# A sparse-expert encoder layer: normalised rows laid out by expert and rank while attention runs, instead of gathered by each expert

## The chip, the cores and the metric

One Trainium2 chip, one core. The metric is the device time of one execution in microseconds (us), median of three runs. The core has five engines that run their own instruction streams: TensorE (PE, matrix products), VectorE (DVE), ScalarE (ACT), GpSimd (POOL) and SyncE (SP), which only issues transfers here. Transfers (DMAs) between device memory and on-chip memory are carried by 16 DMA engines. In the profile, transfers issued by SP run on queue q1, those issued by ACT on q10, and those issued by POOL on q0.

## What is computed

One encoder layer on 2048 tokens of width 1024, in fp32: a gated linear attention group (GLA) and a softmax attention group read the same normalised input, their outputs are projected and added to the residual `h`; then a sparse expert layer with 64 experts. Each token goes to the best of 8 groups and to the best 2 of its 8 experts:

```python
g_idx = jnp.argmax(g_logits, axis=-1)
top_val, top_idx = lax.top_k(e_logits, TOP_K)        # 2 of the group's 8 experts
gate = g_w * jax.nn.softmax(top_val, axis=-1)
expert_id = g_idx[:, None] * EXPERTS_PER_GROUP + top_idx
...
h = jax.nn.silu(xb @ w_gate[e]) * (xb @ w_up[e])     # xb: the expert's rows, normalised
return h @ w_down[e]                                 # scaled by gate, added to the residual
```

So there are 4096 assignments of a token to an expert, 64 per expert on average. A final RMS norm ends the layer.

## The kernel before

All products are split products: an fp32 operand is cut into a rounded part (`fp32r`) and a remainder, and three products stand for one. The program has five stages.

- **Projection** (0 to 292 us of the trace): 16 tiles of 128 tokens are normalised, transposed and projected; results go to scratch tensors in device memory.
- **GLA and row maxima** (to 770 us): a loop `for i in range(NT)` (L780) over the 16 tiles. Tile i projects with `wqk` and `wv`, runs the chunked GLA (`gla`, L694) and one pass of row maxima (`maxpass`, L671). `load_u` (L618) loads the next tile's `uT`, `maxpass` loads its `q1`, and GLA's parts are stored (`d_qe`, `d_X`, `d_oi`). The order on every engine is a scheduler's. The remainder of the weights `wv` and the matrix `K1` are loaded by SP at the stage's start.
- **Attention** (to 1640 us): a planner (`Plan`, L120 on) with cost estimates orders PE, DVE, ACT and POOL; SP's order follows the program and the scheduler. Beside the attention blocks (`key_block`) it places each tile's output projection (`project`, L974), which loads the residual into `h`, adds, stores `d_h`, normalises in place, stores the normalised rows to `d_xn`, computes router logits and calls `route` (L1196). `route` finds a token's two experts `eid`, its rank within each expert (`rk`, from a product with a triangular matrix and a running count `acc`), and its gate. A record of token number and gate is scattered by POOL into `d_list` at the place rank x 64 + expert; the last two tiles' records are put into the on-chip table `L` by products (`list_columns`, L1288). `L` has 100 places (`CAP`) for each of 64 experts. The last tile (`last_rows`, L1141; `last_store`, L1190) is spread over steps of its own.
- **Experts** (1690 to 2895 us): `experts` (L1467) plans 64 experts. Each needs six loads of 1 MB by SP (`raw`: two halves each of gate, up and down weights) into 9 buffers; ACT casts each half (`wh`, L1503), DVE makes the remainder (`wl`, L1505), PE multiplies (`products`, L1554). An expert's rows come by `inputs` (L1511): POOL gathers the rows that `L` names out of `d_xn` into one of two buffers `xg` of 100 rows (L1514), PE transposes them (L1540). The result `o` is added into `d_h` by a POOL scatter-add (`sums`, L1609, issue at L1617). The first five weight loads are made at the end of attention; the sixth waits for the first gather:

```python
raws[n] = next_raw(lambda raw: blocks[e][1](raw, which, half), first[0] if after else None)
```

  `first[0]` is the first gather. Names with unused places: a place of `L` that no token holds names a token out of bounds, and the gather skips it.
- **Finish**: `d_h` is read, normalised and written out. A part that runs only if an expert has more than 100 tokens follows; it does not run with these inputs.

A transfer on SP's queue also waits for the transfer eight places before it on its semaphore (eight such semaphores are used in turn by SP and ACT).

Of the kernel before, what the change touches and what calls it, by code (L numbers as in the profile page):

```python
# [8 lines left out]
F32 = mybir.dt.float32  # L9
F32R = mybir.dt.float32r  # L10
I32 = mybir.dt.int32
# [21 lines left out]
LROWS = NE * CAP  # L33
# [163 lines left out]
def hybrid_encoder_kernel(ctx, tc, x, norm1_gain, w_in, gla_up_fwd, gla_up_fwd_bias, gla_up_bwd,  # L197
# [51 lines left out]
    d_h = scratch("d_h", [T, D])  # L249
    d_list = scratch("d_list", [LROWS + OROWS, 2], I32)  # L250
# [5 lines left out]

    nc.gpsimd.dma_start(d_list[0:LROWS].rearrange("(p a) c -> p (a c)", p=CAP), L.rearrange("p e c -> p (e c)"))

# [331 lines left out]
    with ExitStack() as ph:  # L590
# [25 lines left out]
        tset = tc.keep_in_program_order(nc.scalar.preload_act_table_set("natural_log_exp_and_others"))  # L616

# [162 lines left out]
        for i in range(NT):  # L780
            proj(i)
            if i == 0:
                tc.keep_in_program_order(nc.sync.dma_start(K1.bitcast(F32), d_K1))
            if i + 1 < NT:
                load_u(i + 1)
                decay(i + 1)
            else:

                right.close()
                kvp = right.enter_context(tc.tile_pool(name="pkv", bufs=1, side="right", reuse_waits="tile"))  # L790
                K2 = kvp.tile([DH + 1, NKV, T], F32R, name="K2")
                V = kvp.tile([P, NT, NKV, VW], F32R, name="V")
                nc.sync.dma_start(K2.bitcast(F32), d_K2)
                nc.sync.dma_start(V.bitcast(F32), d_V)
                qp = right.enter_context(tc.tile_pool(name="pcq", bufs=2, side="right", reuse_waits="tile"))
                for kv in range(NKV):
                    load_q(NT - 1, kv)
            g, m = gla(i), maxpass(NT - 1 - i)
            while g or m:
                for n, it in ((1, "g"), (2, "m")):  # L800
                    for _ in range(n):
                        if it == "g" and g and next(g, 0) == 0:
                            g = None
                        if it == "m" and m and next(m, 0) == 0:
                            m = None
# [4 lines left out]
    with ExitStack() as ph:  # L810
# [18 lines left out]
                     "h": 1, "gla": 1, "route": 1, "on": 1, "oa": 1, "w": 0, "mtg": 0})  # L829
# [10 lines left out]
        def rsqrt_steps(dst, ss, n, t0):  # L840

            w = ss.shape[-1]
            hx = sp.tile([P, w], F32, name=f"hx{w}", bufs=4)
            t = sp.tile([P, w], F32, name=f"nt{w}", bufs=4)
# [113 lines left out]
        def load_h(i, t, name, bufs):  # L958
            hs = [sp.tile([P, 512], F32, name=name, bufs=bufs) for _ in range(2)]
            for j in range(2):  # L960
                nc.sync.dma_start(hs[j], x2[i * P:(i + 1) * P, j * 512:(j + 1) * 512])
            return hs, landed(t)

        def load_h(i, t, name, bufs):
            hs = [sp.tile([P, 512], F32, name=name, bufs=bufs) for _ in range(2)]
# [8 lines left out]
        def project(i, t):  # L974
# [60 lines left out]
            th = t  # L1035
            for b in range(2):
# [4 lines left out]
                if b == 1:  # L1041
                    give((t[0] + 2.5, "dma"), "h")
# [16 lines left out]
            yield from route(i, lg, t)  # L1059
# [81 lines left out]
        def last_rows(t):  # L1141
# [7 lines left out]
            tx, xs = [], []  # L1149
            for j in range(2):  # L1150
# [4 lines left out]
                tx.append((yield ask("dve", 0.6, t, take=("den",))))  # L1155
                xs.append(sp.tile([P, 512], F32, name="den"))
# [31 lines left out]
            yield from route(i, lg, t)  # L1188
# [7 lines left out]
        def route(i, lg, t):  # L1196
# [53 lines left out]
            t = yield ask("dve", 0.5, t)  # L1250
# [4 lines left out]
            give(t, "pt")  # L1255
            v.tensor_tensor(acc, acc, ob, op=OP.add)
            give(t, f"rank{i - 1}")
            if i in order[-2:]:
# [7 lines left out]
                give(t, "route", "p")  # L1266
                return

            t = yield ask("dve", 0.1, t, tg)
            di = sp.tile([P, 2], I32, name="di", bufs=2)  # L1270
            v.scalar_tensor_tensor(di, rk, float(NE), eid, op0=OP.mult, op1=OP.add)
            give(t, "route")
            for k in range(2):
                t = yield ask("pool", 1.04, t)
# [6 lines left out]
            if i == order[-3]:  # L1281
                t = yield ask("pool", 1.04, t)
                nc.gpsimd.dma_start(L, d_list[0:LROWS].rearrange("(p e) c -> p e c", p=CAP))
                t = yield ask("dve", 0.15, landed(t, 5.0))
                v.tensor_copy(L0, L[:, :, 0])
# [86 lines left out]
        listed = []  # L1372
        last_h, raw_pools, ahead, taken = [], [], [], [0]

        def next_raw(load, after=None):
# [3 lines left out]
            ld = load(raw)  # L1379
            if after is not None:  # L1380
                tc.add_manual_dep(ld.ins, after.ins.name, mybir.DependencyInfo(
                    mybir.DependencyClass.Sync, mybir.DependencyReason.DATA), reason="the first rows go before")
# [31 lines left out]
    with ExitStack() as ph:  # L1414
# [6 lines left out]
        for t in xgs:  # L1421
            nc.gpsimd.memset(t, 0.0)
# [44 lines left out]
        def experts(blocks, ahead=(), then=None):  # L1467
# [3 lines left out]
                         "hh": 2, "o": 2, "visit": NG, "raw": NAHEAD + NB - len(ahead), "issued": 0, "landed": 0})  # L1471
# [11 lines left out]
            def loads():  # L1483
                for n, (e, which, half) in enumerate(seq):
# [3 lines left out]
                    else:  # L1488
                        after = ahead and n == len(ahead)
                        t = yield ask("dma", 2.6, take=("raw", "landed") if after else ("raw",))  # L1490
                        raws[n] = next_raw(lambda raw: blocks[e][1](raw, which, half), first[0] if after else None)
                    give((t[0] + 2.0, "dma"), f"raw{n}")

            def weights(n):
# [11 lines left out]
                if n == 0:  # L1506
                    tc.add_manual_dep(lo.ins, first[1].ins.name, data_dep, reason="the first rows go before")
# [3 lines left out]
            def inputs(e):  # L1511
                xg = xgs[e % 2]
                t = yield ask("pool", 1.95, listed_at, take=("xg",), urge=20.0)
                get = nc.gpsimd.indirect_dma_start(  # L1514
                    out=xg, out_offset=None, in_=d_xn, in_offset=bass.IndirectOffsetOnAxis(ap=column(e, 0), axis=0),
                    bounds_check=T - 1, oob_is_err=False)
                if e == 0:
                    first.extend((get, nc.gpsimd.memset(issued, 0.0)))
                    give(t, "issued")
                t = yield ask("dma", 0.8, (t[0] + 1.5, "pool"), urge=20.0)  # L1520
                if e + 1 < nb:
                    add(inputs(e + 1))
                tx = t[0] + 1.8, "dma"
                if e == 0:
                    give(tx, "landed")
# [112 lines left out]
        with tc.manual_schedule(engines={mybir.EngineType.PE, mybir.EngineType.DVE, mybir.EngineType.Activation,  # L1638
                                         mybir.EngineType.Pool} | ({mybir.EngineType.SP} if SPM & 2 else set())):
            t = experts([(L[:, e], lambda raw, which, half, e=e: load_expert(e, raw, which, half)) for e in expert_order],  # L1640
# [22 lines left out]
        with tc.If(nblk_v > 0):  # L1663
# [19 lines left out]
            with tc.For_i(0, nblk_v, 1) as b:  # L1683
# [9 lines left out]
                experts([(Lb, load)])  # L1693
# [32 lines left out]
```

## Time and profile before

| | |
|---|---|
| median of three runs | 2981.13 us (2977.4 to 2981.16) |
| profiled execution, own time | 2981.33 us |
| its span, first to last instruction | 2979.4 us |
| PE busy | 2812.6 us (94%) |
| DVE, ACT, POOL busy | 75%, 62%, 15% |
| moved by DMA | 647.00 MB, mean 217 GB/s |
| of it queue q1 (SP) | 590.92 MB, 54.3% of 16 engines' span |
| of it queue q0 (POOL) | 34.36 MB, 5.3% |

A share of an engine over the whole span is a mean over stages with different limits, so the rows further down are taken stage by stage. "DMA share" is the mean busy share of the 16 DMA engines, with 1.00 for all busy all the time. PE's granted clock is a share of full speed.

### The profile page before, as it was taken

Reading aid. Unit: us, or ns where it says so; the run is one execution under the profiler, and the core shown is the slowest. Engines: PE = TensorE matmul, PEld = TensorE weight load, DVE = VectorE, ACT = ScalarE, POOL = GpSimd, SP = SyncE. Lnnn points to the kernel's source line nnn. Section 1 sums busy time; section 2 is a strip of 40 time slices with the busy share of each in tenths; the row PEclk is TensorE's granted clock in tenths of the full one; section 3 lists DMA queues with packets and bytes.
Section 4 is the critical chain, followed back from the end, with each engine's and each line's share of the span. In section 5 each row is a group of like instructions: output and inputs, shape, how many; then the busy total and the mean of one; then the engine's idle time right before and its main releaser. Section 6 shows DMA issues by size and latency. Waiting matters only on the chain.

```text
span 2979.4 us, 38648 instructions
## 1 busy us (share of the span) xinstructions
PE 2812.6 (94%) x13776; PEld 2101.0 (71%) x13776; DVE 2225.4 (75%) x3222; ACT 1852.0 (62%) x2776; POOL 448.4 (15%) x326
## 2 busy tenths in 40 slices
PE   7999899999999999999999799999999999999992
PEld 6888688887677777777776566676676666666771
DVE  6655688888676677776666788888788878778783
ACT  4433333333677777777776567777777777777773
POOL 3433111111000000000000121111111112122111
PEclk9999999999899999999999899999999999999996
DMA  7884422233521121121221799999999999999986
GB/s 254 283 279 162 149 105 91 94 105 118 198 66 63 63 80 59 61 80 58 66 77 42 249 371 365 358 355 353 352 364 353 354 353 357 350 345 357 353 311 236
DMA packets 175140, 647.00 MB, mean 217 GB/s; under 512 B 38885, under 2 KB 53575, under 8 KB 119325
## 3 DMA queue, kind: packets, MB, share of 16 engines
q1 hardware_dynamic: 136766, 590.92, 54.3%
q0 software_dynamic: 23712, 34.36, 5.3%
q10 hardware_dynamic: 14464, 19.21, 2.0%
q8 instruction: 109, 1.79, 0.2%
q14 instruction: 89, 0.73, 0.1%
HBM read 546.08 MB, written 117.13 MB: 223 GB/s over the span
## 4 chain that ended last, share of the span: by engine, by line
PE 59%; DMA 21%; issue 7%; DVE 6%; ACT 5%; POOL 1%; ACTq 0%; SPq 0%; POOLq 0%; DVEq 0%
DMA raw<-in_w_gate_dram 10%; DMA raw<-in_w_up_dram 7%; PE pm L1007 6%; PE pm L681 4%; PE pa L1356 4%; PE ps L1328 4%; PE pa L1354 4%; PE pa L1355 4%; PE py L1575 4%; PE pg L1569 4%; PE ps L1329 4%; PE pv L334 3%; PE pqk L334 3%; DVE wl L1505 2%; ACT wh L1503 2%
## 5 line engine op out<-in xcount | busy, mean ns | idle before, releaser
L1505 DVE TENSOR_TENSOR wl<-raw,wh 128x2048 fp32r<-128x2048 f32 x384 | 873.5, 2289 | 218.2 <-ACT wh L1503 215.6
L1503 ACT CAST wh<-raw 128x2048 fp32r<-128x2048 f32 x384 | 727.0, 1908 | 272.5 <-DMA raw<-in_w_up_dram 146.9
L1343 DVE TENSOR_TENSOR p_l<-p,p_h 128x512 fp32r<-128x512 f32 x512 | 343.8, 689 | 199.4 <-ACT p_h L1340 193.1
L1332 ACT ACTIVATE p<-ps 128x512 f32<-128x512 f32 x512 | 296.4, 599 | 150.0 <-PE ps L1329 129.4
L683 DVE TENSOR_REDUCE nm<-pm 128x1 f32<-128x1024 f32 x256 | 304.9, 1216 | 46.7 <-PE pm L681 46.5
L1569 PE MATMUL pg<-wh,xT 128*100 128x512 f32 x1024 | 335.4, 398 | 0.0
L1569 PE MATMUL pu<-wh,xT 128*100 128x512 f32 x1024 | 330.7, 394 | 0.0
L1575 PE MATMUL py<-wh,hT 128*100 128x512 f32 x1024 | 320.7, 416 | 0.0
L1340 ACT CAST p_h<-p 128x512 fp32r<-128x512 f32 x448 | 269.0, 624 | 5.8
L1514 POOL DMA_INDIRECT xg<-d_xn,L x64 | 109.2, 1707 | 914.6 <-PE pt L1540 904.5
L1569 PEld LDWEIGHTS pu<-wh,xT 128*100 128x100 f32 x1024 | 168.1, 164 | 68.2
L1569 PEld LDWEIGHTS pg<-wh,xT 128*100 128x100 f32 x1024 | 170.7, 167 | 64.6
L1328 PE MATMUL ps<-q,K 128*128 128x512 f32 x512 | 210.6, 411 | 1.2 <-ACT p L1332 0.8
L1575 PEld LDWEIGHTS py<-wh,hT 128*100 128x100 f32 x1024 | 170.3, 176 | 55.6
L1354 PE MATMUL pa<-p_h,V 128*66 128x512 f32 x512 | 204.3, 399 | 0.0
L1356 PE MATMUL pa<-p_l,V 128*66 128x512 f32 x512 | 202.6, 396 | 0.9 <-DVE p_l L1343 0.9
L1329 PE MATMUL ps<-q,K 65*128 65x512 f32 x512 | 203.2, 397 | 0.0
L1569 PE MATMUL pg<-wl,xT 128*100 128x512 f32 x512 | 202.0, 395 | 0.0
L1355 PE MATMUL pa<-p_h,V 128*64 128x512 f32 x512 | 201.4, 393 | 0.0
L1569 PE MATMUL pu<-wl,xT 128*100 128x512 f32 x512 | 200.5, 392 | 0.0
L681 PE MATMUL pm<-K,q 128*128 128x512 f32 x512 | 169.6, 416 | 1.1 <-DVE nm L683 1.1
L1575 PE MATMUL py<-wl,hT 128*100 128x512 f32 x512 | 166.3, 407 | 0.0
(415 smaller groups left out, 5041.9 us busy)
## 6 DMA issues: line engine op xcount, KB each, us to landing
raw<-in_w_gate_dram SPq DMA_DIRECT2D x128, 1024.0 KB
raw<-in_w_up_dram SPq DMA_DIRECT2D x128, 1024.0 KB
raw<-in_w_down_dram SPq DMA_DIRECT2D x128, 1024.0 KB
d_uT<-uT SPq DMA_DIRECT2D x16, 1024.0 KB
uT<-d_uT SPq DMA_DIRECT2D x15, 1024.0 KB
x_t<-in_x_dram SPq DMA_DIRECT2D x16, 512.0 KB
wraw<-in_w_in_dram SPq DMA_DIRECT2D x32, 256.0 KB
d_q<-q ACTq DMA_DIRECT2D x16, 512.0 KB
```

The lines of the kernel that those rows point to most:

```text
L683: nc.vector.tensor_reduce(nm[:, h, b:b + 1], pm, axis=AX.XY, op=OP.max, negate=True)
L1328: nc.tensor.matmul(ps, lhsT=K1[:, kv, ks], rhs=r1, start=True, stop=False)
L1329: nc.tensor.matmul(ps, lhsT=K2[:, kv, ks], rhs=r2, start=False, stop=True)
L1332: nc.scalar.activation(p, ps, AF.Exp)
L1343: nc.vector.tensor_tensor(p_l, p, p_h.bitcast(F32), op=OP.subtract)
L1354: nc.tensor.matmul(pa, lhsT=hi, rhs=p_h, start=(kt == 0), stop=False)
L1355: nc.tensor.matmul(pa[0:DH], lhsT=V[:, kt, kv, 0:DH], rhs=p_h, start=False, stop=False)
L1356: nc.tensor.matmul(pa, lhsT=hi, rhs=p_l, start=False, stop=(kt == NT - 1))
L1503: nc.scalar.copy(wh, raw)
L1505: lo = nc.vector.tensor_tensor(wl, raw, wh.bitcast(F32), op=OP.subtract)
L1569: nc.tensor.matmul(acc_p, lhsT=xTs[e][:, a, k, :], rhs=w[:, kk, :], start=(k == 0 and a == 0 and w is wh), stop=(k == KD - 1 and a == 1))
L1575: nc.tensor.matmul(acc_p[:, c], lhsT=hTs[e][:, a, k, :], rhs=w[:, kk, c * 512:(c + 1) * 512], start=(k == 0 and a == 0 and w is wh), stop= ...
```

## The change

While attention runs, POOL writes each token's normalised row twice to a new tensor `d_xs` in device memory, at row rank x 65 + expert (`spread`, 32 scatters of 128 rows). An expert's 100 places are then a strided block of `d_xs`, which SP loads with two plain transfers (96 and 4 rows), in place of POOL's gather. Since unused places would hold whatever memory held, `d_xs` is filled with zeros first: 51 stores of 512 KB out of a small tile of zeros, written in the GLA loop. The residual tile `h` gets a second buffer, since the scatter reads it until it has landed. `d_xn`, `d_list` and `L` stay (`L` still names the tokens for the scatter-add, and holds the gates); the number of experts in the place's stride goes from 64 to 65 (`NE1`). The sixth weight load has no hand-made wait any more. The diff, cut to its core:

```diff
+    d_xs = scratch("d_xs", [XROWS, D])
+    places = lambda a: a[0:LROWS].rearrange("(p e) c -> p e c", p=CAP)
...
+        zero = wp.tile([P, 1, D // 4], F32, name="zero")
+        nc.gpsimd.memset(zero, 0.0)
+        empty = list(range(0, XROWS, P))
...
+            for _ in range(-(-len(empty) // (NT - i))):
+                r0 = empty.pop()
+                nc.sync.dma_start(d_xs[r0:r0 + P].rearrange("p (a d) -> p a d", a=4), zero.to_broadcast([P, 4, D // 4]))
...
-                     "h": 1, "gla": 1, "route": 1, "on": 1, "oa": 1, "w": 0, "mtg": 0})
+                     "h": 2, "gla": 1, "route": 1, "on": 1, "oa": 1, "w": 0, "mtg": 0})
...
+            di = sp.tile([P, 2], I32, name="di", bufs=3)
+            v.scalar_tensor_tensor(di, rk, float(NE1), eid, op0=OP.mult, op1=OP.add)
+            add(spread(i, di, xn, t, tg))
...
+        def spread(i, di, xn, t, tg):
+
+            for k in range(2):
+                t = yield ask("pool", 1.1, t, take=() if k else (f"xn{i}",))
+                st = nc.gpsimd.indirect_dma_start(
+                    out=d_xs, out_offset=bass.IndirectOffsetOnAxis(ap=di[:, k:k + 1], axis=0), in_=xn, in_offset=None,
+                    bounds_check=LROWS - 1, oob_is_err=False)
...
+            if i != last:
+                give(landed(t, 6.0), "h")
...
-        for t in xgs:
-            nc.gpsimd.memset(t, 0.0)
+        xs_of = places(d_xs)
...
-                        t = yield ask("dma", 2.6, take=("raw", "landed") if after else ("raw",))
-                        raws[n] = next_raw(lambda raw: blocks[e][1](raw, which, half), first[0] if after else None)
+                        t = yield ask("dma", 2.6, take=("raw", "rows") if after else ("raw",))
+                        raws[n] = next_raw(lambda raw: blocks[e][1](raw, which, half))
...
-                t = yield ask("pool", 1.95, listed_at, take=("xg",), urge=20.0)
-                get = nc.gpsimd.indirect_dma_start(
-                    out=xg, out_offset=None, in_=d_xn, in_offset=bass.IndirectOffsetOnAxis(ap=column(e, 0), axis=0),
-                    bounds_check=T - 1, oob_is_err=False)
...
+                    t = yield ask("dma", 1.0, listed_at, take=("xg",), urge=20.0)
+                    for c0, c1 in ((0, 96), (96, CAP)):
+                        nc.sync.dma_start(xg[c0:c1], xs_of[c0:c1, place])
```

The order on the engines moves at three places. The first is SP's queue at the start of the GLA stage; `wraw` are the weights `wv`, `K` is `K1`, `q` is `q1`. Before:

```order
L427 DMA d_sg<-sg 128x512 x2
L299 DMA wraw<-in_w_in_dram 128x512 x8
L783 DMA K_3219<-d_K_84 128x4096
L620 DMA uT<-d_uT 128x2048
L628 DMA zT<-d_zT 98x128
L674 DMA q_3442<-d_q_96 128x1024
```

and with the change:

```order
L432 DMA d_sg<-sg 128x512 x2
L808 DMA d_xs<-zero 512x1x256 x3
L304 DMA wraw<-in_w_in_dram 128x512 x8
L808 DMA d_xs<-zero 512x1x256 x2
L791 DMA K_3220<-d_K_84 128x4096
L628 DMA uT<-d_uT 128x2048
L636 DMA zT<-d_zT 98x128
L682 DMA q_3449<-d_q_97 128x1024
```

Three stores of zeros come ahead of the loads of `wv` and two more ahead of `K1`; all 51 stand within the first six tiles, 11 for each tile from the third on, not spread over 16 as the loop's text has them.

The second is SP's queue from the end of attention into the experts; `p` is the last tile's residual, `den` its normalised rows. Before:

```order
L1370 DMA raw<-in_w_gate_dram 128x2048
L1154 DMA d_h<-p 128x512 x2
L1194 DMA d_xn<-den 128x512 x2
L1370 DMA raw<-in_w_gate_dram 128x2048
L1370 DMA raw<-in_w_up_dram 128x2048 x2
L1370 DMA raw<-in_w_down_dram 128x2048 x2
```

and with the change:

```order
L1395 DMA raw<-in_w_gate_dram 128x2048
L1203 DMA d_xn<-den 128x512 x2
L1395 DMA raw<-in_w_gate_dram 128x2048
L1395 DMA raw<-in_w_up_dram 128x2048
L1544 DMA xg_18240<-d_xs 96x1024
L1544 DMA xg_18240<-d_xs 4x1024
L1544 DMA xg_18241<-d_xs 96x1024
L1544 DMA xg_18241<-d_xs 4x1024
L1395 DMA raw<-in_w_up_dram 128x2048
L1544 DMA xg_18240<-d_xs 96x1024
```

The sixth and seventh weight loads stand ahead of the first expert's rows, and later ones behind them; from the fifth expert on each two gate halves are followed by the rows of the expert after the next, then by two up and two down halves.

The third is POOL over the same place; `rec_a` are records, `di` places. Before:

```order
L1275 DMA d_list<-rec_a,di 10400x2 x28
L1283 DMA L<-d_list 100x128
L1193 TENSOR_SCALAR den<-den,rsh 128x512 x2
L1430 IOTA thr 64x20
L1514 DMA xg_18102<-d_xn,L 100x1024
L1518 MEMSET issued 1x1
```

and with the change:

```order
L1286 DMA d_xs<-h,di 6528x1024 x2
L1299 DMA d_list<-rec_a,di 10500x2 x2
L1307 DMA L<-d_list 100x128
L1286 DMA d_xs<-h,di 6528x1024 x2
L1202 TENSOR_SCALAR den<-den,rsh 128x512 x2
L1286 DMA d_xs<-den,di 6528x1024 x2
L1451 IOTA thr 64x20
L1550 MEMSET issued 1x1
L1645 DMA d_h<-o,L 2048x1024 x64
```

The scatters of rows are interleaved with those of records during attention, the last tile's two come right before the experts, and of the 64 gathers none is left between the 64 scatter-adds.

## Rows read from the trace of the kernel before

**Rows 1.** Busy by stretch: us, PE, PEld, DVE, ACT, POOL, PE clock, DMA share, GB/s
```profile
330.00:770.00 440.00, 434.51 (x2352) 347.58 (x2352) 387.65 (x497) 143.12 (x273) 63.80 (x46) 0.98 0.28 97
770.00:1640.00 870.00, 866.30 (x4296) 620.14 (x4295) 601.08 (x1530) 648.85 (x1423) 29.25 (x29) 1.00 0.24 77
1640.00:1690.00 50.00, 31.04 (x170) 24.41 (x169) 33.48 (x107) 22.03 (x46) 10.42 (x9) 0.78 0.57 208
1690.00:2895.00 1205.00, 1149.48 (x5246) 834.51 (x5245) 978.61 (x634) 869.75 (x686) 219.08 (x122) 0.98 1.00 356
```

**Rows 2.** Chain that ended last, shares of the span by engine
```profile
PE 59%; DMA 21%; issue 7%; DVE 6%; ACT 5%; POOL 1%; ACTq 0%; SPq 0%; POOLq 0%; DVEq 0%
```

**Rows 3.** Waits between 1690 and 2895 us: in total, times, longest
```profile
PE pt L1599 <- DVE hh L1593: 44.6, 18, 3.6
```

**Rows 4.** Timeline and chain, PE: where products of an expert's gate weights start
```profile
1688.05 0.73 PE L1569 MATMUL pg<-wh,xT 128*100 128x512 f32 x1
...
1994.10 5.53 PE pg L1569 x24
...
2012.00 5.54 PE pg L1569 x24
...
2900.00 0.39 PE L1569 MATMUL pg<-wh,xT 128*100 128x512 f32 x1
```

**Rows 5.** DMA queues, 1750 to 2750 us: packets, MB, share of 16 engines
```profile
q1 hardware_dynamic: 45026, 327.86, 87.0%
q0 software_dynamic: 18238, 27.20, 12.4%
```

**Rows 6.** DMA queues in 1705:1712, 1690:1697 (two rows), 2862:2871, 2871:2878, 2066:2076, 779:788
```profile
q1 hardware_dynamic: 401, 2.92, 100.9%
...
q1 hardware_dynamic: 258, 1.86, 87.3%
q0 software_dynamic: 176, 0.31, 16.0%
...
q1 hardware_dynamic: 500, 3.63, 100.3%
...
q1 hardware_dynamic: 311, 2.24, 85.4%
...
q1 hardware_dynamic: 437, 3.15, 89.6%
...
q1 hardware_dynamic: 1286, 3.52, 102.7%
```

**Rows 7.** DMA queue of ACT over the span: packets, MB, share of 16 engines
```profile
q10 hardware_dynamic: 14464, 19.21, 2.0%
```

**Rows 8.** Timeline, GLA stage: start us, us, instruction [idle before, who ended it]
```profile
301.05 3.85 SPq L299 DMA_DIRECT2D wraw<-in_w_in_dram  x8
...
304.56 0.79 PE L334 MATMUL pv<-wvh,u 128*128 128x512 f32 x1 [6.08 <-ACT wvh L289]
...
350.40 0.32 SPq L620 DMA_DIRECT2D uT<-d_uT  x1
...
378.65 0.40 PE L334 MATMUL pqk<-wqkh,uT 128*128 128x512 f32 x1
```

**Rows 9.** Timeline and chain around the last tile's routing; a quiet scatter-add and load
```profile
10.17 2.40 DMA wraw<-in_w_in_dram
...
1674.70 0.22 DVE L1254 SCALAR_TENSOR_TENSOR prz<-pt,o12z 128x64 f32<-128x64 f32 x1
...
1678.32 1.19 POOL L1514 DMA_INDIRECT xg<-d_xn,L  x1 [7.03 <-DVE L L1306]
...
1683.82 0.33 SPq L1370 DMA_DIRECT2D raw<-in_w_gate_dram  x1
1683.85 1.60 PE L1540 MATMUL pt<-cst_sb,xg 100*128 100x100 f32 x8 [6.71 <-DMA xg<-d_xn,L]
...
2918.64 6.76 DMA d_h<-o,L
```

More of the change, by code (lines that the diff above doesn't have):

```diff
@@ L32 @@
 FE = 512
-LROWS = NE * CAP
+NE1 = NE + 1
+LROWS = NE1 * CAP
+XROWS = -(-LROWS // P) * P
 OBLK = 2 * T // CAP
@@ L958, in load_h @@
         def load_h(i, t, name, bufs):
[L959 to L965, printed above, removed]
+            if name == "h":
+                h = sp.tile([P, D], F32, name="h", bufs=2)
+                hs = [h[:, j * 512:(j + 1) * 512] for j in range(2)] + [h]
+            else:
+                hs = [sp.tile([P, 512], F32, name=name, bufs=bufs) for _ in range(2)]
             for j in range(2):
@@ L1035, in project @@
             th = t
+            give(t, f"xn{i}")
             for b in range(2):
@@ L1148, in last_rows @@
             tr = yield from rsqrt_steps(ra, s1, 512, t)
-            tx, xs = [], []
+            tx = []
+            xn = sp.tile([P, D], F32, name="den", bufs=1)
+            xs = [xn[:, j * 512:(j + 1) * 512] for j in range(2)]
             for j in range(2):
@@ L1194, in last_store, with route @@
                 nc.sync.dma_start(d_xn[last * P:(last + 1) * P, j * 512:(j + 1) * 512], xs[j])
-        def route(i, lg, t):
+            give(t, f"xn{last}")
+        def route(i, lg, t, xn):
             own = "z" if i == last else ""
@@ L1265, in route @@
                 t = yield from list_columns(i, o12, at, vals, t, tg)
-                give(t, "route", "p")
+                give(t, "p")
+            give(t, "route")
+        def spread(i, di, xn, t, tg):
[4 more added lines that the diff above has]
+                    bounds_check=LROWS - 1, oob_is_err=False)
+                for x in spreads:
+                    tc.declare_no_dep(st.ins, x.ins, reason="every assignment has a row of its own")
+                spreads.append(st)
+            if i != last:
+                give(landed(t, 6.0), "h")
+            if i in order[-2:]:
                 return
[L1269 to L1272, printed above, removed]
+            rec = rec_a[:, i]
             for k in range(2):
-                t = yield ask("pool", 1.04, t)
+                t = yield ask("pool", 1.04, t, tg)
                 st = nc.gpsimd.indirect_dma_start(
@@ L1370, in load_expert, with next_raw @@
             return nc.sync.dma_start(raw, v[:, half * 2048:(half + 1) * 2048])
-        listed = []
+        listed, spreads = [], []
         last_h, raw_pools, ahead, taken = [], [], [], [0]
-        def next_raw(load, after=None):
+        def next_raw(load):
             pool = raw_pools[len(raw_pools) > 1 and taken[0] % (NAHEAD + NB) >= NAHEAD]
@@ L1378, in next_raw @@
             raw = pool.tile([P, 2048], F32, name="raw")
[L1379 to L1382, printed above, removed]
+            load(raw)
             return raw
@@ L1470, in experts @@
             plan = Plan({"xg": 2, "xT": 2, "hT": 2, "wh": WN, "wl": WN, "pt": 2, "pg": 1, "pu": 1, "py": PYN,
-                         "hh": 2, "o": 2, "visit": NG, "raw": NAHEAD + NB - len(ahead), "issued": 0, "landed": 0})
+                         "hh": 2, "o": 2, "visit": NG, "raw": NAHEAD + NB - len(ahead), "issued": 0, "rows": 0})
             add, give = plan.add, plan.give
@@ L1505, in weights @@
                 lo = nc.vector.tensor_tensor(wl, raw, wh.bitcast(F32), op=OP.subtract)
-                if n == 0:
-                    tc.add_manual_dep(lo.ins, first[1].ins.name, data_dep, reason="the first rows go before")
+                if n == 0 and first:
+                    tc.add_manual_dep(lo.ins, first[0].ins.name, data_dep, reason="the last rows go to their places first")
                 ws[n] = wh, wl
@@ L1639, in hybrid_encoder_kernel @@
                                          mybir.EngineType.Pool} | ({mybir.EngineType.SP} if SPM & 2 else set())):
-            t = experts([(L[:, e], lambda raw, which, half, e=e: load_expert(e, raw, which, half)) for e in expert_order],
+            t = experts([(L[:, e], lambda raw, which, half, e=e: load_expert(e, raw, which, half), e) for e in expert_order],
                         ahead, count_blocks)
@@ L1692, in load @@
                     nc.sync.dma_start(raw, v[:, half * 2048:(half + 1) * 2048])
-                experts([(Lb, load)])
+                experts([(Lb, load, None)])
             finish()
```

40 lines of the change are left out of this document (23 added, 17 removed).

## The prediction, made before the changed kernel was timed

> **What bounds the kernel now.** I read the busy times by stretch first, then the queues, then the places of the edits. Up to 1640 us PE sets the time: it is busy 434.51 of 440 us in most of the GLA stage and 866.30 of 870 us in attention, with a DMA share of 0.28 and 0.24 [rows 1]. From 1690 to 2895 us the DMA engines have a share of 1.00 at 356 GB/s, while PE is still busy 95% of the time [rows 1], and the chain that ended last has 59% PE and 21% DMA [rows 2]. Both are near their limit there, so the next question is the pace. From the first product of an expert's gate weights to that of the 64th lie 2900.00 - 1688.05 = 1211.95 us, 63 periods of 19.24 us on the mean; a period in which PE waited for nothing took 2012.00 - 1994.10 = 17.90 us [rows 4]. So the transfers set the mean, and PE stands 1.34 us below it: whatever the change takes off the transfers, it gets no more than 63 x 1.34 = 84 us here. The largest waits of PE are for `hh`, 44.6 us in all [rows 3]; that is the gate and up products' end, which comes late when a weight load did.
>
> What fills the transfers' time: between 1750 and 2750 us q1 moved 327.86 MB [rows 5], or 312.7 loads of 1.0486 MB, six for an expert, so 52.1 experts, 19.2 us each. POOL's queue took 12.4% of the engines' time [rows 5], 124 us / 52.1 = 2.38 us for an expert's gather and scatter-add together. The change takes the gather out of that and puts a plain load in.
>
> **The experts: what a gather costs.** Three looks, since the queue's own packets may not be all it takes. First, a gather alone beside weight loads (1690 to 1697 us): its packets took 16.0% of 7 us = 1.12 us of all engines [rows 6]. Second, what q1 lost there: it moved 1.86 MB in 7 us [rows 6]. With POOL's queue silent it moved 2.92 MB in 7 us, 3.63 in 9 and 3.15 in 10 [rows 6], that is 0.417, 0.403 and 0.315 MB/us, mean 0.378. So it lost 7 - 1.86 / 0.378 = 2.08 us, or 2.54 by the fastest rate. Third, a scatter-add alone left q1 2.24 MB in 7 us [rows 6], a loss of 1.07 us, and a period of 19.24 us less 6.29 MB / 0.378 = 16.64 leaves 2.60 us for both, so 1.5 for the gather. I take 1.6 us, the middle of 1.12 and 2.08; the ends for the range are 1.12 and 2.54.
>
> **What the plain load costs.** All 100 places come, 0.4096 MB, about 36 of them empty, in rows of 4 KB like the gather's. Plain loads with such rows, early in the GLA stage, moved 3.52 MB in 9 us, 0.391 MB/us [rows 6], so 1.05 us; by the slowest silent rate, 0.315, it is 1.30 us. If rows are dealt to 16 engines, 96 give six each and the last four make a seventh, where the mean is 6.25: up to 7 / 6.25 = 1.12 times as much, 1.46 us. I take 1.2 us; the ends are 1.05 and 1.46.
>
> Net: 1.6 - 1.2 = 0.4 us for an expert, and 62 of them in the steady stage: **-25 us**. At the ends, 2.54 - 1.05 = 1.49 us, of which PE lets 1.34 through, so -83 us; and 1.12 - 1.46 = -0.34, a loss of 21 us.
>
> The loads now stand in SP's queue between weight loads. The load for the expert after the next may issue only when PE has transposed the rows two experts earlier, and weight loads queue behind it. PE does that a whole period before the rows are wanted, and some 5 MB of weights are in flight or landed ahead by then, since nine buffers of 1 MB are there; I cost this wait at nothing. If the cover is gone, it is a stall of the transfers of at most the time from a free buffer to PE's transposes, and the time is again that of the third rival below. POOL is left with the scatter-adds; they do not start sooner, since they wait for the experts' outputs.
>
> **From routing into the experts.** Before: the last rank stands at 1674.70, the list goes through PE and DVE, POOL issues the first gather at 1678.32, PE's transposes start at 1683.85 and the sixth weight load issues at 1683.82 [rows 9]. After: the place is one more DVE operation (about 0.2 us as the row of 1674.70), then POOL issues two scatters of rows, at 1.19 us each [rows 9], so at about 1677.3. A quiet scatter-add takes 6.76 us from issue to landing [rows 9]; this one moves 128 rows instead of 64, so I take no less, 1683.9. The load of the first rows follows, 2.40 us as a quiet 256 KB load [rows 9]: 1686.3, so PE starts 2.5 us later. Against that the sixth and seventh weight loads no longer wait for a gather. Two loads are 2.10 MB, 5.5 us at 0.378 MB/us, moved into a stretch whose DMA share is 0.57 [rows 1], and the stage behind it is bound by transfers. Ends: -5.5 (all of it is kept) and +2.5 (none of it). I take **-2 us**.
>
> **The zeros.** 51 stores of 524,288 bytes, 26.7 MB. They run beside PE's GLA work, except for the first five. Three stand ahead of the loads of `wv` in SP's queue and two ahead of `K1`. Before, these loads issue at 301.05, and PE waits 6.08 us for their cast [rows 8], so there the transfer is on the path. No row shows a store in pieces of 1 KB. The nearest price is ACT's queue, which moves pieces of 1.3 KB: 2.0% of 16 engines over 2979.4 us for 19.21 MB [rows 7], 953 engine-us, 0.322 MB/us for all 16. Three stores are then 4.9 us, all five 8.1. Below nothing is excluded, as nothing becomes shorter here. The ends are 0 (the loads overtake the stores on other engines, or the stores go out while PE has earlier work) and 8.1; I take **+5 us**, since PE has no cover at this place. The other 46 go out 11 to a tile: 46 x 0.524 / 0.322 = 75 us of all engines, in four to five tiles. A tile lasts about 28 us (`uT` is loaded at 350.40 and first used at 378.65 [rows 8], one tile on), and the engines are idle 72% of it [rows 1], about 20 us a tile, where 11 stores take 18. That is tight, but `uT` has 28 us of slack: cost nothing. If that cover goes, each of four tiles may lose what 11 stores miss, some 2 us, 8 us in all.
>
> **Attention.** 30 scatters of 128 rows and their places. POOL is busy 29.25 of 870 us, and 30 x 1.19 = 36 us more leave it idle; 30 x 0.524 MB at 77 GB/s of traffic so far [rows 1] fit in a DMA share of 0.24. The residual tile is held until the scatter has landed, which is what its second buffer is for. PE is idle 3.7 us in all of attention, so nothing can be gained, and the extra DVE operations of about 0.2 us lie on an engine with 35% [rows 1] to spare or more. Nothing.
>
> **The sum** is made against the profiled execution, 2981.33 us, which is the median (2981.13) within 0.2 us: 2981.3 - 25 - 2 + 5 = **2959 us**. Its own range, with the costs at moderate values (the experts -0.1 to -0.8 us each, the rest -5 to +8), is 2935 to 2975.
>
> **Rivals.** *The empty rows decide (slower).* In this stage what counts is bytes: the transfers run at 356 GB/s with a share of 1.00 [rows 1], and 36 empty places of 100 add 36 x 4096 x 64 = 9.4 MB, 26.5 us at that rate. With +5 for the zeros it gives 3012 us. It decides from the point where a gather takes no more than its 64 rows' bytes, 0.262 MB / 0.356 = 0.74 us, against 1.15 for the load. For it: the rate of the whole stage. Against it: q1 alone ran at 417 GB/s in 1705 to 1712 us [rows 6], so 356 is no ceiling, and a gather's own packets already took 1.12 us for 0.31 MB. [...] Chance 0.18.
>
> *PE becomes the bound.* The gather cost over 2 us and the load 1 or less, so the period falls to 17.90. That gives 2981 - 84 + 5 = 2902 us. For it: the loss of 2.08 us in q1 [rows 6]; against it: the packets' 1.12, and that slow stretches such as 0.315 come with POOL's queue silent too, so that part of 19.24 has nothing to do with gathers. Chance 0.12.
>
> *A wash.* What the gather gives back (1.3, say) the load takes again, or SP's wait for free `xg` buffers does, and the zeros remain: 2981 + 0 to +5, less 2 to 6, so 2975 to 2997. For it: 1.12 against 1.05 to 1.46 at the low end of one and the high end of the other. Chance 0.20.
>
> **How the numbers follow.** The forecast has 0.50. A measurement of this kernel can tell about 0.2% (6 us) from no change. Faster by more than that: the forecast and the second rival, 0.62. Within it: 0.14, most of the wash. Slower: the first rival and the rest of the wash, 0.06, so 0.24. The range from 2900 to 3000 takes in all but the first rival, so that 0.18 is left out.
>
> **What would show it.** Right: a period between first gate products near 18.8 us, a share of POOL's queue near 6% instead of 12.4, more megabytes of q1 in 1000 us (some 7% for the rows alone and 2% for the pace), the first product of an expert within 3 us of 1688 plus the zeros' delay, and a wait of PE for `wvh` some 5 us longer than 6.08. Wrong: a period at 19.2 or above with POOL's queue at 6% (the bytes count, or SP's queue waits behind the load of rows, which the waits of SP for PE's transposes would show); a period at 17.9 (PE bounds). GLA tiles longer than 28 us from the third to the sixth would show that the zeros had no cover.

## The result and the profile after

The changed kernel takes 3020.07 us (median of 4 runs, 3016.3 to 3023.36) against 2981.14 us before: a ratio of 1.0132, interval 1.0114 to 1.0149. That is 39 us slower, above the range of the prediction, which had 2959.

By stretch (us, PE, PEld, DVE, ACT, POOL, PE clock, DMA share, GB/s), to be held against [rows 1]:

```profile
330.00:770.00 440.00, 434.63 (x2357) 347.68 (x2355) 388.71 (x498) 142.87 (x272) 63.73 (x46) 0.99 0.43 148
770.00:1640.00 870.00, 866.86 (x4291) 620.92 (x4292) 600.75 (x1535) 648.12 (x1427) 61.48 (x57) 1.00 0.28 94
1640.00:1690.00 50.00, 29.01 (x167) 22.33 (x166) 26.77 (x98) 14.34 (x37) 7.38 (x8) 0.79 0.75 264
1690.00:2895.00 1205.00, 1129.20 (x5087) 810.17 (x5086) 951.61 (x618) 850.76 (x670) 120.29 (x59) 0.97 0.97 348
```

In GLA and attention PE is as busy as before; the DMA share rose with the zeros and scatters, and so did POOL's time in attention (61 us, before 29). In the experts PE has less work done in the same time (1129 against 1149 us), and the transfers are slower, 348 against 356 GB/s.

Where products of the first and of the 64th expert's gate weights start, on PE's timeline:

```profile
1691.49 0.73 PE L1597 MATMUL pg<-wh,xT 128*100 128x512 f32 x1
...
2940.03 0.39 PE L1597 MATMUL pg<-wh,xT 128*100 128x512 f32 x1
```

The mean period is (2940.03 - 1691.49) / 63 = 19.82 us, against 19.24 from [rows 4]. So 0.58 x 63 = 36.6 us of the loss lie in the steady stage and 1691.49 - 1688.05 = 3.4 us ahead of it; together 40.0, and the two profiled spans differ by 3019.5 - 2979.4 = 40.1.

The 3.4 us, from the timelines of PE and DVE at GLA's start and at the last rank, to be held against [rows 8, 9]:

```profile
305.84 0.80 PE L339 MATMUL pv<-wvh,u 128*128 128x512 f32 x1 [6.46 <-ACT wvh L294]
...
1676.01 0.23 DVE L1264 SCALAR_TENSOR_TENSOR prz<-pt,o12z 128x64 f32<-128x64 f32 x1
```

`wv`'s products start 1.3 us later than before, and the last rank stands 1.3 us later too, so nothing was lost between them. From the last rank to the first gate product it is now 15.5 us, before 13.4: 2.1 us more.

The queues between 1750 and 2750 us (packets, MB, share of 16 engines), and what SP waited for from 1690 to 2895 us (total, times, longest):

```profile
q1 hardware_dynamic: 49074, 334.17, 90.1%
q0 software_dynamic: 8804, 13.25, 6.9%
```

```profile
SPq L1544 <- PE pt L1568: 627.6, 62, 16.1
SPq L1395 <- DMA raw<-in_w_gate_dram: 231.9, 83, 4.1
```

POOL's queue fell from 12.4% [rows 5] to 6.9%, as forecast, while SP's rose from 87.0% to 90.1%. So the DMA engines now stand idle for nearly 3% of the time, and before for almost none. By the trace's packet records (an expert has 768 weight packets, so 52.1 experts pass in these 1000 us before and 49.9 now) an expert takes 0.87 us longer in this window (0.58 over all 63 periods). Its rows' own packets on q1 are 100 x 262 ns / 16 = 1.64 us; POOL's queue takes 1.00 us less, the weight packets 0.29 us less (347 ns on the mean before, 341 now), and the engines are idle 0.5 us more. The loss against the kernel before thus stands in the rows' own packets and in idle engines, not in slower weight packets.

SP now stands 10 us in each period at the load of rows, waiting for PE's transposes with the weight loads behind it. That wait was my first suspect.

### The profile page after: what moved, and what is told of

Read it like the earlier page. It is cut to its first block, busy times and chain, and to the rows that moved or that the text cites. A ratio compares the mean times of both kernels' runs of the same rounds, so it can differ in the third digit from the quotient of the medians.

```text
span 3019.5 us, 38798 instructions
## 1 busy us (share of the span) xinstructions
PE 2828.7 (94%) x13776; PEld 2101.2 (70%) x13776; DVE 2224.4 (74%) x3224; ACT 1854.1 (61%) x2776; POOL 381.8 (13%) x293
## 4 chain that ended last, share of the span: by engine, by line
PE 55%; issue 16%; DMA 16%; ACT 5%; DVE 4%; POOL 2%; SPq 1%; ACTq 0%; POOLq 0%; DVEq 0%
DMA raw<-in_w_up_dram 11%; PE pm L1016 6%; PE pm L689 4%; PE pa L1379 4%; PE pa L1381 4%; PE ps L1353 4%; PE pa L1380 4%; PE ps L1354 3%; PE pv L339 3%; PE pqk L339 3%; PE pg L1597 2%; PE py L1603 2%; PE pu L1597 2%; DMA raw<-in_w_gate_dram 2%; ACT wh L1524 2%
## 5 line engine op out<-in xcount | busy, mean ns | idle before, releaser
L1597 PE MATMUL pg<-wh,xT 128*100 128x512 f32 x1024 | 347.2, 410 | 0.0
L1603 PE MATMUL py<-wh,hT 128*100 128x512 f32 x1024 | 314.2, 409 | 0.0
L1645 POOL DMA_INDIRECT d_h<-o,L x64 | 128.2, 2003 | 1160.3 <-ACT o L1640 1121.4
L1597 PEld LDWEIGHTS pg<-wh,xT 128*100 128x100 f32 x1024 | 177.0, 173 | 68.4
```

What stands on the lines that cost most here:

```text
L1597: nc.tensor.matmul(acc_p, lhsT=xTs[e][:, a, k, :], rhs=w[:, kk, :], start=(k == 0 and a == 0 and w is wh), stop=(k == KD - 1 and a == 1))
L1603: nc.tensor.matmul(acc_p[:, c], lhsT=hTs[e][:, a, k, :], rhs=w[:, kk, c * 512:(c + 1) * 512], start=(k == 0 and a == 0 and w is wh), stop= ...
```

## The experiments

Times are medians; before ran beside each at 2980.6 to 2981.4 us.

### What the parts cost

**Rows gathered as before, all else of the change kept.** Edit: `None` in place of the expert's place, so that `inputs` takes the gather, and the two buffers are cleared as before.

> The changed kernel with the experts' rows gathered by POOL as before; zeros, scatters of rows during attention and the sixth weight load without its wait stay. It gives what all of the change but the plain loads costs. Prediction by its parts: +5 for the zeros, 0 for attention, -5.5 to +2.5 at the experts' start: 2979 to 2989. If the loss of the changed kernel lies in the plain loads (both theories Q and B), it is within 6 us of 2981; if contention in attention or the zeros cost more, it shows here.

2982.58 us, ratio 1.0005 (0.9996 to 1.0015). The zeros, the scatters and the free sixth load together cost nothing that can be told. The whole loss is the plain loads'.

**The kernel before without its gathers, and the changed one without its loads of rows.**

```diff
+                if e < 2:
                     get = nc.gpsimd.indirect_dma_start(out=xg, ..., in_=d_xn, ...)
```
```diff
-                    for c0, c1 in ((0, 96), (96, CAP)):
+                    for c0, c1 in ((0, 96), (96, CAP)) if e < 2 else ():
```

> The kernel before, but only the first two experts' rows are gathered (left out: the gathers of 62 experts). It gives the whole price of a gather beside weight loads. The prediction's 1.6 us would bring the period from 19.24 to its floor of 17.9 (PE), 83 us less: 2898. By its packets alone (1.12 us): 2912. By its bytes alone (0.262 MB at 0.356 MB/us, 0.74 us): 2935.

> The changed kernel, but only the first two experts' rows are loaded; the others multiply what the two buffers hold (left out: the loads of rows of 62 experts). It gives the whole price of the plain loads, bytes and SP's waits together. Theory B: 0.41 MB at 0.348 MB/us, 1.18 us for each of 62, 73 us: 2947. Theory Q: bytes plus a dry stretch of about 0.6 us a period, 1.7 us, which PE at 17.9 us a period just lets through (1.9 us a period): 2915 or so.

2890.95 and 2896.71 us. The stretch from 1750 to 2750 us without gathers, then without loads of rows:

```profile
1750.00:2750.00 1000.00, 1000.00 (x4694) 737.04 (x4693) 877.31 (x567) 780.71 (x614) 88.95 (x56) 1.00 1.00 367
```

```profile
1750.00:2750.00 1000.00, 1000.00 (x4694) 737.09 (x4694) 877.82 (x569) 780.87 (x615) 88.80 (x56) 1.00 1.00 367
```

PE is busy all the time in both, so both are at PE's floor, and what was taken out costs at least the difference: 89.6 / 62 = 1.45 us for a gather, 123.4 / 62 = 1.99 us for a plain load of rows, SP's wait for it included. The gather's price was forecast well (1.6); the load's (1.2) was not.

**The kernel before without the sixth load's wait** (`next_raw` without `first[0]`).

> The kernel before without the hand-made wait of the sixth weight load for the first gather. The prediction's term for the experts' start: up to 5.5 us less (2975.6); if the first gather comes later behind the load, up to 2.5 us more.

2975.18 us, 0.9985 (0.9975 to 0.9994): 5.4 us less, with an interval from 2 to 7. What a free sixth load gives back was of the right size, 5.5 us at most.

### Theory Q: SP's queue waits behind the rows

**The rows issued by POOL** (`nc.gpsimd.dma_start` in place of `nc.sync.dma_start`).

> The changed kernel with one edit: the plain loads of an expert's rows are issued by POOL instead of SP. Bytes, rows and waits for PE's transposes stay; only SP's queue of weight loads no longer stands behind them. Theory Q (SP's weight loads wait behind the load of rows for PE's transposes, 609 us in all, and the DMA engines run dry): SP's wait for PE's transposes is gone, the DMA share goes from 0.97 back to 1.00, and of the 39 us lost against before at least 20 come back: 3000 us or less. Theory B (the 36 empty rows of each load cost their bytes): no change beyond 6 us of 3020.

2980.08 us, ratio 1.0003: all of it came back, and the engines were busy all the time (1750 to 2750 us):

```profile
1750.00:2750.00 1000.00, 954.93 (x4375) 690.02 (x4374) 814.10 (x530) 723.95 (x571) 157.10 (x156) 0.99 1.01 364
```

That spoke for Q, but the edit changes more than the wait: the rows also move to another queue, where an expert's two loads bring about 44 packets of 4 bytes (16640 on q0 between 1750 and 2750 us; 52 scatter-adds of 176 packets and the 52 x 100 rows leave 2288) and on SP's queue 20, so they are not cut up alike.

**Three buffers.**

```diff
-        xgs = [... for j in range(2)]
+        xgs = [... for j in range(3)]
-                xg = xgs[e % 2]
+                xg = xgs[e % 3]
```

> The changed kernel with three buffers for an expert's rows instead of two, so that a load of rows may issue a whole expert earlier. Theory Q: the wait of SP for PE's transposes shrinks from about 10 us a period to near none if the load keeps its place in SP's queue, time 3000 us or less. If the planner moves the load forward with the buffer, SP waits as long as before and the time stays at 3020: then it tells nothing of Q. Theory B: 3020 in either case.

> The changed kernel with three buffers for rows in place of two, but with the planner told of two, so that in the steady stage the load of rows keeps its place in SP's queue and waits for PE's transposes of one expert earlier. Same queue, same bytes, same transfers as the changed kernel; only the wait goes. Theory Q: SP's wait for PE's transposes (609 us) falls under 50, the DMA share goes to 1.00 and the time to about 2980, as with POOL's issue. Theory B, or a price of SP's plain rows against POOL's: 3010 or more.

With the planner told of three it moved the load forward; SP waited 671 us for PE and the time was 3017.76: it tells nothing, as that expectation allows. With the planner told of two, it was 3040.46 us, slower. SP's waits from 1690 to 2895 us, and the stretch from 1750 to 2750 us, of that kernel:

```profile
SPq L1395 <- DMA raw<-in_w_up_dram: 298.8, 113, 5.3
SPq L1395 <- DMA raw<-in_w_gate_dram: 292.7, 108, 4.9
SPq L1395 <- DMA raw<-in_w_down_dram: 284.4, 113, 3.9
```

```profile
1750.00:2750.00 1000.00, 917.38 (x4107) 654.79 (x4106) 768.35 (x499) 683.33 (x537) 96.18 (x49) 0.97 1.00 343
```

The wait for PE is gone, the DMA share is 1.00 as forecast, and yet only 343 GB/s move, less than the 348 of the changed kernel. **Theory Q fell as the cause of the loss:** the engines are all busy and slow. The idle stretches were there, but taking the wait away did not give their time back; what they cost in the changed kernel is not told apart.

### Theories B and M: the bytes, or where the rows lie

**64 rows, with and without SP's wait, and from the upper places.**

```diff
-                    for c0, c1 in ((0, 96), (96, CAP)):
+                    for c0, c1 in ((0, 60), (60, 64)) if e > 1 else ((0, 96), (96, CAP)):
```

> The changed kernel, but from the third expert on only the first 64 of the 100 places are loaded (60 and 4 rows); rows of places 64 to 99 are left out, so the computed sums differ where an expert has more than 64 tokens. Theory B: 0.147 MB less for each of 62 experts at 0.348 MB/us is 0.42 us each, 26 us in all: 2994 us. Theory Q: SP still waits behind the load of rows and the transfers still run dry; less than 10 us come back: 3010 or more.

> The same with only 64 of the 100 rows loaded from the third expert on (places 64 to 99 left out). Against the run with 64 rows and SP's wait (2935) it gives the price of the wait where the rows are fewer. If the wait costs the same at any number of rows: 2935 - 40 = 2895, PE's floor. If the wait only costs where transfers are already late (a feedback: late weights, late transposes, later loads): within 10 us of 2935, and the 85 us between 100 and 64 rows shrink to some 50 without the wait (0.147 MB x 62 at 0.36 MB/us is 25).

> The kernel with 64 rows (60 and 4), but taken from places 36 to 99 instead of 0 to 63; they land in the same 64 partitions (left out: places 0 to 35). Theory M in another form: the upper, mostly empty places lie in memory that is slower to read; then 2960 or more. Theory P or B, where only number and dealing of rows count: 2935 within 8 us.

2935.47, 2933.41 and 2936.31 us. 36 rows less give 85 us, more than three times what their bytes take at 348 GB/s (26 us); SP's wait makes no difference there, nor do the places from which the rows come.

**Rows that lie side by side** (and `places` reads in the same order).

> The changed kernel with the places laid out the other way round: expert x 100 + rank in place of rank x 65 + expert, so that an expert's 100 rows are one contiguous block of memory instead of rows 266 KB apart (valid where no expert has more than 100 tokens, as here). Theory M: the distance of the rows in memory makes their packets slow; then 4 KB packets fall from 262 ns to 180 or less and the time to 2990 or less. Theory P or B: 3020 within 8 us.

```diff
-            v.scalar_tensor_tensor(di, rk, float(NE1), eid, op0=OP.mult, op1=OP.add)
+            v.scalar_tensor_tensor(di, eid, float(CAP), rk, op0=OP.mult, op1=OP.add)
```

3034.65 us, 15 us slower where M wanted 30 faster and P or B the same time; why it is slower is open. The distance of the rows in memory is not the cause; M fell in both forms.

### Theory P: how a transfer's rows are dealt to the engines

The packet counts gave the lead. Beside its rows a transfer has packets of 4 bytes: a store of 128 rows that ran alone at 1369 us in the changed kernel had 128 packets of 2 KB and 16 of 4 bytes. From 1750 to 2750 us the changed kernel had 5784 of these on q1 for 299 weight loads and 50 loads of rows: 299 x 16 + 50 x 20 = 5784. The 20 I split into 16 for 96 rows and 4 for 4 rows, since the run with one transfer of 96 fits 16 (49226 packets and 337.24 MB on q1 leave about 5660; 303 weight loads and 50 of rows: 353 x 16 = 5648). One transfer of 100 rows has 10 (5183 for 293 and 49: 293 x 16 + 49 x 10 = 5178), and 60 rows have 15 (the 50874 packets and 352.03 MB on q1 of 60 + 4 leave 6178 for 322 weight loads and 54 loads of rows: 322 x 16 + 54 x 19 = 6178). I read the number as that of the engines that a transfer uses; no view names the engine that a packet ran on.

**Other cuts of the 100 rows.**

> The changed kernel with an expert's rows loaded by one transfer of 100 rows in place of 96 and 4. Theory Q: one place less in the eight of SP's semaphores, the wait for PE's transposes as before: within 6 us of 3020. If the split of rows over the engines matters (7 rows at the busiest instead of 6.25 on the mean), up to 0.12 x 1.1 = 0.13 us an expert either way, 8 us.

> The changed kernel, but from the third expert on only 96 rows are loaded, by one transfer (places 96 to 99 left out). The profile's packet counts say that a transfer of 96 rows is dealt to 16 engines (6 rows each) and one of 4 rows to 4 engines, which then carry 7. If bytes matter alone: 1 MB less in all, 3 us: 3017. If the most loaded engine sets a period: one row of 4 KB less at it, about 0.16 us an expert (29 us / 62 / 3 rows, from 10 rows against 7 in the two forms measured): 3010. With one place less in SP's eight semaphores nothing else is expected.

> The changed kernel with an expert's 100 rows in three transfers of 64, 32 and 4 rows instead of 96 and 4: all rows come, but 64 of them are dealt 4 to an engine as in the run with 64 rows, and 32 are dealt 2 to an engine. Theory P: the dealing of 6 to an engine, which straddles the weight loads' groups, is gone for two thirds of the rows: 2965 to 3000. Theory B: 3020, or up to 10 us more for the third transfer.

One transfer of 100: 3049.15. One of 96: 3006.75, 13 us for four rows. 64 + 32 + 4: 3052.62, where P as I had it forecast a gain. So small even shares are not what helps, and neither is the number of transfers (one of 100 is slower than 96 + 4, one of 96 is faster).

**128 rows in one transfer, and the same 128 in two.** The tile gets 128 partitions and `d_xs` 128 places for each expert; 28 are never used. The edits, cut to their core:

```diff
-XROWS = -(-LROWS // P) * P
+XROWS = NE1 * P
-        xgs = [wp.tile([CAP, D], ...) for j in range(2)]
+        xgs = [wp.tile([P, D], ...) for j in range(2)]
-                    for c0, c1 in ((0, 96), (96, CAP)):
-                        nc.sync.dma_start(xg[c0:c1], xs_of[c0:c1, place])
+                    nc.sync.dma_start(xg, xs_of[:, place])
```
```diff
-                    nc.sync.dma_start(xg, xs_of[:, place])
+                    for c0, c1 in ((0, 64), (64, P)):
+                        nc.sync.dma_start(xg[c0:c1], xs_of[c0:c1, place])
```

> The changed kernel, but an expert's rows come as one transfer of 128 rows (places 0 to 127, of which the upper 28 are never used) into a tile of 128 partitions; d_xs has 128 places for each expert, filled with zeros (65 stores instead of 51). Theory P: packets slow each other down where a transfer's rows are dealt to the 16 engines in another way than the weight loads' 128 rows; of 100 rows a 4 KB packet took 262 ns in the changed kernel, of 64 rows 218 ns. With 128 rows the dealing is that of the weight loads, 8 rows to an engine: packets of about 160 ns, and although 0.115 MB more come for each expert the time is under 2995. Theory B (bytes): 0.115 x 62 / 0.348 = 20 us more than 3020, 3040.

> The kernel with 128 rows (2925), but the same 128 rows of the same places come in two transfers of 64 rows, each dealt 4 rows to an engine, instead of one of 128 dealt 8 to an engine like the weight loads. Same bytes, same packets, 8 rows for each engine in all. Theory P (what counts is that an engine writes the same partitions as in the weight loads): the gain is gone, 4 KB packets take 250 ns or more and the time is 3000 or more. If it is only that every engine gets the same number of rows: 2925 within 10 us.

2925.05 us (ratio 0.9811, 0.9793 to 0.9829) and 3089.77 us (1.0375, 1.0349 to 1.0401): the same rows and bytes, 165 us apart. Against the changed kernel the one transfer moves 0.115 MB more for each expert and is 95 us faster.

The six us after SP issues a load of rows (packets, MB, share of 16 engines), first the changed kernel (2001.1 to 2007.1), then one transfer of 128 (2013.8 to 2019.8), then two of 64 (2017.4 to 2023.4):

```profile
q1 hardware_dynamic: 299, 1.77, 98.6%
```

```profile
q1 hardware_dynamic: 389, 2.33, 97.2%
q0 software_dynamic: 3, 0.01, 0.7%
```

```profile
q1 hardware_dynamic: 281, 1.53, 98.5%
```

The 16 engines are nearly full in each of the three, and the bytes are 1.77, 2.33 and 1.53 MB. Over all loads of rows between 1750 and 2750 us these six us have 1.69, 2.17 and 1.54 MB on the mean, each with a share near 0.95. The packets themselves take longer. Out of the trace's packet records on q1, 1750 to 2750 us:

```
rows of an expert        time us   4 KB packets   8 KB weight packets
                                   mean ns        mean ns   90th percentile
96 + 4 (changed)         3020      262            341       439
100 in one               3049      249            343       466
64 + 32 + 4              3053      282            345       426
96 + 4, third buffer     3040      228            363       489
60 + 4                   2935      218            329       327
60 + 4, third buffer     2933      181            342       379
64 + 64                  3090      287            354       516
128 in one               2925      200            315       324
128 in one, third buffer 2903      160            321       321
gathered (before)        2981      -              347       408
96 + 4 issued by POOL    2980      -              345       426
none loaded              2897      -              341       324
```

With the same number of buffers, rows that come otherwise than 128 in one have slower packets of their own. And beside them many weight packets are slow: the 90th percentile is 426 to 516 ns with 96 rows and more and 327 or 379 with 60 + 4, against 324 or 321 with 128 in one and 324 without rows. The mean alone misleads: it is 341 without any loads of rows too, because one packet in twenty takes over 500 ns, while PE is busy all the time and nothing is lost by it.

From 64 + 64 to 128 in one: 768 weight packets of an expert x (354.4 - 315.1) ns / 16 = 1.89 us, and 128 x (287.3 - 200.0) / 16 = 0.70 us, 2.58 us for each of 62 experts: 160 of the 165 us measured. As the engines have shares of 0.99 (128 in one) and 0.98 (64 + 64), such a sum must come near the whole; it tells which packets became longer, not why:

```profile
1750.00:2750.00 1000.00, 982.43 (x4569) 714.49 (x4568) 852.81 (x554) 760.10 (x597) 103.50 (x54) 1.00 0.99 384
```

```profile
1750.00:2750.00 1000.00, 895.13 (x3969) 636.70 (x3968) 737.11 (x480) 659.57 (x517) 100.43 (x47) 0.97 0.98 334
```

From the changed kernel to 128 in one the same sum gives 1.26 x 62 = 78 of 95 us, nearly all of it in the weight packets.

**Why stays open.** That packets slow each other where a transfer's rows are dealt to the engines in another way than the weight loads' 128 is theory P, my conjecture; no run here shows which engine carries which row, or what a slow packet waits for. The pair of 128 against 64 + 64 (2925 and 3090 us) is as P would have it. The cheap 60 + 4 (2935) speaks against it as the whole account, since its 15 and 4 packets of 4 bytes are not the 16 of 128 rows either. The slow forms all have rows that go to partitions 64 and up, and 60 + 4 has none; no run separates this from their larger number of rows.

**The third buffer on top of 128 rows.**

> The kernel with 128 rows in one transfer, and a third buffer that takes SP's wait for PE's transposes away as in the run that gave 3040. If that wait costs nothing where the transfers are fast enough: within 6 us of 2925. If it holds the weight loads up a little: down to PE's floor, 2897.

2903.37 us, ratio 0.9742 (0.9725 to 0.9758), with no part of the work left out. SP's longest waits from 1690 to 2895 us, and the stretch from 1750 to 2750 us:

```profile
SPq L1395 <- DVE wl L1526: 396.2, 199, 4.6
SPq L1395 <- DMA raw<-in_w_up_dram: 203.9, 84, 4.5
```

```profile
1750.00:2750.00 1000.00, 996.83 (x4664) 730.70 (x4663) 870.21 (x564) 775.21 (x609) 95.58 (x55) 1.00 1.01 392
```

PE is busy 997 of 1000 us at 392 GB/s: this beats both kernels and stands 7 us above the kernel without any loads of rows. SP waits for free weight buffers again, not for PE. So the wait at the head of SP's queue did have a price, 22 us, once the rows were cheap. Why its removal made the changed kernel 20 us slower stays open; its weight packets are slower then (363 against 341 ns), which would fit rows that now always run beside weights.

## Why the prediction was wrong

**The step that failed** is the price of the plain load. I bounded it by 1.05 and 1.46 us, from bytes over the rate of plain loads with 4 KB rows [rows 6] and a share for the seventh row. Its own packets alone are 1.64 us of the engines, and with SP's wait for it, which I had put at nothing, it costs at least 1.99. Net, an expert lost 0.58 us where -0.4 was forecast: 36.6 us against -25, the whole miss. The row I took was the wrong kin: a 4 KB packet took 163 ns in that stretch, and one of an expert's rows 262 ns in the changed kernel. The transfers issued in the stretch (779 to 788 us; the prediction puts it in the GLA stage, it is attention's start) are these:

```profile
wol<-d_wo SPq DMA_DIRECT2D x1, 512.0 KB
o<-d_oi SPq DMA_DIRECT2D x1, 256.0 KB
sg<-d_sg SPq DMA_DIRECT2D x1, 256.0 KB
X<-d_X SPq DMA_DIRECT2D x2, 128.0 KB
KB<-d_X SPq DMA_DIRECT2D x2, 128.0 KB
```

`wol`, `o` and `sg` have 128 rows, and most of what ran there was like them. I matched the size of a row, and even that in part (589 of the packets had 4 KB, 539 had 2 KB: `o` and `sg` have rows of 2 KB), and not the number of rows. I even asked how 96 and 4 rows are dealt to 16 engines, and priced the dealing by the fullest engine alone, with no thought that the packets themselves could take longer.

**The gather** (1.6 us, ends 1.12 and 2.54) was right: at least 1.45, with PE's floor beneath.

**SP's wait** "at nothing" failed too: the cover I named was not there. I argued that PE transposes a whole period ahead, and SP waits 628 us for it, while the engines stand idle 0.5 us more for an expert. With cheap rows the wait costs 22 us. In the changed kernel its price is open: without it the engines are busy all the time and the kernel is 20 us slower.

**Zeros** (+5, ends 0 and 8.1): 1.3 us at `wv`, and the GLA tiles stayed at PE's pace, with a DMA share near 0.9 for three tiles (378 to 406 us is one):

```profile
378.00:406.00 28.00, 27.99 (x156) 22.71 (x155) 24.86 (x33) 9.45 (x18) 4.18 (x3) 1.00 0.91 302
```

**The experts' start** (-2; ends -5.5 and +2.5): the first gate product came 2.1 us later, as the part of it on PE's path said (2.5); whether the changed kernel keeps what the free sixth load gives back, 5.4 us in the run of it alone, cannot be read beside the larger loss behind it. **Attention** at nothing: right.

**The rivals.** "The empty rows decide" gave 3012, within 8 us of the result, and its mechanism is wrong: 28 more unused rows made it 95 us faster (128 in one). It was the only rival in which a plain load is clearly dearer than a gather, at 0.18; a time that fits does not show a cause. Its rate, 356 GB/s for the stage, is no ceiling: 392 GB/s ran for 1000 us.

## What to carry to other kernels

Price a new transfer by a row of the trace with the same number of rows, not only the same bytes in a row: in a stage bound by transfers, a load that is cut in another way than the stream beside it can take longer for each byte and hold that stream up too, as 64 + 64 against 128 did (4 KB packets of 287 against 200 ns, the stream's of 354 against 315). It need not, as 60 + 4 shows (218 ns, and 329 of the stream's, 2935 us); a run tells. Where a tile has 100 rows and the stream has 128, try 128: here 28 useless rows bought 95 us. A DMA share of 1.00 says that engines are busy, not that they are fast (here it went with 343 GB/s and, at 1.01, with 392); read GB/s beside it.

## What the runs showed of the hardware

A transfer of 128 rows had 16 packets of 4 bytes, one of 96 rows 16, one of 100 rows 10, one of 60 rows 15, one of 4 rows 4. The same 128 rows of 4 KB took 200 ns a packet in one transfer and 287 ns in two of 64, and 8 KB packets of the weight loads took 315 ns on the mean beside the one and 354 ns beside the two (90th percentile 324 and 516). Transfers moved 392 GB/s for 1000 us on one core, 377 of it SP's loads. The 96 and 4 rows cost 40 us less when POOL issued them (2980) than when SP did (3020); whether SP's free queue or the other cut made that is open.
